# Seven block products for eight in the value projections of a dilated attention

## The chip, the cores and the metric

The kernel runs on one core of one Trainium2 chip. The metric is the time of one execution on the device in microseconds; it is the median of three runs, and less is better.

## The reference

A trunk of two layers over 256 tokens of width 1024, all in float32. Layer 0 mixes the tokens by neighbourhood attention and latent attention, layer 1 by dilated attention; a squared-ReLU MLP follows each. The change lies in layer 1. Cut to it:

```python
def odd_mixer(xn, w_in, w_o, cos_f, sin_f):
    b, s, _ = xn.shape
    hcat = (xn @ w_in).reshape(b, s, DIL_GROUPS, 3, DIL_HEADS, HEAD_DIM)   # 3 groups, q/k/v, 16 heads of 64
    q = apply_rope(hcat[:, :, :, 0], cos_f, sin_f)
    k = apply_rope(hcat[:, :, :, 1], cos_f, sin_f)
    v = hcat[:, :, :, 2]
    return dilated_attention(q, k, v) @ w_o

# dilated_attention: for each group (w, d) of ((128, 1), (512, 4), (2048, 16)) a query attends to the keys
# at offsets -w/2 .. w/2 in steps of d; the three results are combined by their softmax denominators.
```

So each head needs its queries, keys and values in three groups, all of them products of the same normed activations (256 x 1024) with columns of `w_in`.

## The kernel before, in words

A float32 product is made of three faster ones. Each operand is split in two: a high part (`split`: ScalarE casts to float32r, L205) and a low part (VectorE subtracts, L206); `mm3` then adds high x high, high x low and low x high (L209 to L211). Weights come from memory by SP's DMA queue into `raw` tiles (four buffers, `RAWBUFS`), are split in `WPARTS` pieces into `whi` and `wlo` (three buffers each), and are used. `specs` lists all weight tiles in order of use; `weight()` hands out the next one, after it has begun loads up to `LOAD_AHEAD` tiles ahead and splits up to `SPLIT_AHEAD` tiles ahead.

Layer 1 works in eight units of two heads. A unit has three tiles of query and key weights and two of value weights. `qk_steps` makes the query and key products (L927, L928), evacuates them (L934, L935) and applies rope: four DMAs on SP's queue swap halves (`sw`, L942), then VectorE multiplies by cosine (L947) and sine (L948) and adds (L950, L953). Part b = 0 gives the queries and keys of the first group (`q0h`, `q0l`), b = 1 the queries of the other two (`q12`), b = 2 their keys (`k12`). `value_steps` makes the values of the three groups for two blocks of 128 tokens, 384 columns wide and eight blocks of 128 inputs deep: 2 x 8 x 3 matmuls of 128x384. VectorE writes the first group's values (`v0`, L904), ScalarE those of the other two (`v12`, L907, L908).

`attention` of a unit has the scores of the first group (`two_heads`, L218), the strided scores (L981), the softmax (L992 to L997), and transposes (L1004). `mix` multiplies with the values (L1019, L1024). `weave` runs the products of unit u as `main`, with the attention of unit u - 1 as `side` between its steps. A scheduler then sets the order on each engine from this program; each engine runs its own list strictly in that order and waits for the others by semaphores.

The MLPs make their second product by seven products of blocks for eight (`SEVEN`): weights are summed in blocks by DMAs that add to what lies there (POOL's queue, L145) and activations are combined on VectorE.

## Time and profile before

| | |
|---|---|
| median of the runs | 733.81 us (733.56 to 734.0, 3 runs) |
| the profiled execution, its own time | 734.39 us |
| its span in the profile | 732.6 us |
| granted TensorE clock | 0.999 |
| busy in the span: TensorE, VectorE, ScalarE, POOL | 99%, 85%, 71%, 10% |
| moved by DMA | 149.56 MB, 204 GB/s over the span |

A row of an instruction group gives the line, the engine, what is written and read, the shape, the number, then the busy time in us and the mean duration of one in ns, and behind the second bar the idle time ahead of it and what ended that. Rows of TensorE and VectorE can overlap their neighbours by a part of their duration, so the distance from start to start is what one costs. A row of waits has the total in us, the number of times and the longest.

### The profile page before, as it was taken

What the parts mean: (1) busy time and instruction counts of PE and PEld (TensorE: products, weight loads), DVE (VectorE), ACT (ScalarE), POOL (GpSimd) and SP (SyncE); (2) the same over time, 40 slices, a digit from 0 to 9 for tenths busy, and PEclk for the clock granted to TensorE, in tenths of its full rate; (3) what the DMA queues carried; (4) which work ended last, traced back from release to release, by engine and by line L of the source; (5) the groups of instructions that cost most, each with busy time, mean ns of one, the idle gap of its engine ahead of it and who ended that gap; (6) DMA issues with size and microseconds to landing.
All of it is one profiled execution on the core that took longest, in us unless ns stands there. A gap on an engine that the chain in (4) does not pass through costs nothing.

```text
span 732.6 us, 13831 instructions
## 1 busy us (share of the span) xinstructions
PE 723.4 (99%) x5234; PEld 661.0 (90%) x5234; DVE 623.7 (85%) x1188; ACT 521.8 (71%) x985; POOL 75.8 (10%) x73
## 2 busy tenths in 40 slices
PE   9999999999999999999999999999999999999995
PEld 6988899999999998989899899998999999999995
DVE  6888859999999959988777888788759998999956
ACT  7778968767767756877676766867658766776851
POOL 0100002224212000000000000000003132222000
PEclk9999999999999999999999999999999999999999
DMA  8773338799888644664655456455558797898601
GB/s 314 278 260 135 116 115 216 214 283 249 264 265 231 218 160 166 216 211 149 223 181 176 167 187 212 167 187 200 204 190 201 242 271 217 259 272 241 217 32 59
DMA packets 38212, 149.56 MB, mean 204 GB/s; under 512 B 5121, under 2 KB 6657, under 8 KB 29057
## 3 DMA queue, kind: packets, MB, share of 16 engines
q1 hardware_dynamic: 30240, 133.71, 51.6%
q0 software_dynamic: 7616, 14.68, 12.1%
q8 instruction: 41, 0.67, 0.4%
q10 hardware_dynamic: 288, 0.28, 0.1%
q14 instruction: 27, 0.21, 0.1%
HBM read 142.10 MB, written 1.05 MB: 195 GB/s over the span
## 4 chain that ended last, share of the span: by engine, by line
PE 82%; issue 10%; DVE 4%; ACT 1%; DMA 1%; POOL 0%; POOLq 0%; ACTq 0%; DVEq 0%
PE acc L927 11%; PE acc L209 10%; PE acc L210 9%; PE w L209 9%; PE w L210 9%; PE acc L211 9%; PE w L211 9%; PE acc L928 5%; PE w L218 1%; PE w L1004 1%; DVE wlo L206 1%; PE acc L1019 1%; PE w L806 1%; DMA sum<-in_w 1%; PE w L820 1%
## 5 line engine op out<-in xcount | busy, mean ns | idle before, releaser
L206 DVE TENSOR_TENSOR wlo<-raw,whi 128x512 fp32r<-128x512 f32 (+3 forms) x360 | 297.3, 847 | 51.9 <-ACT whi L205 51.8
L205 ACT CAST whi<-raw 128x512 fp32r<-128x512 f32 (+3 forms) x360 | 253.5, 746 | 87.2 <-PE w L210 58.9
L210 PE MATMUL w<-xx,whi 128*128 128x256 f32 x528 | 149.6, 283 | 0.2
L211 PE MATMUL w<-xx,wlo 128*128 128x256 f32 x528 | 149.3, 283 | 0.0
L209 PE MATMUL w<-xx,whi 128*128 128x256 f32 x528 | 148.9, 283 | 0.0
L927 PE MATMUL acc<-xx,whi 128*128 128x512 f32 x336 | 122.1, 404 | 0.0
L210 PEld LDWEIGHTS w<-xx,whi 128*128 128x128 f32 x528 | 101.2, 192 | 1.7 <-DVE xx L246 0.6
L209 PEld LDWEIGHTS w<-xx,whi 128*128 128x128 f32 x528 | 101.0, 192 | 1.1
L211 PEld LDWEIGHTS w<-xx,wlo 128*128 128x128 f32 x528 | 101.2, 192 | 0.0
L928 PE MATMUL acc<-xx,wlo 128*128 128x256 f32 x336 | 94.4, 281 | 0.0
L144 POOL COPY sum<-sum 128x512 f32<-128x512 f32 x28 | 39.3, 1417 | 463.6 <-DMA sum<-in_w 406.6
L927 PEld LDWEIGHTS acc<-xx,whi 128*128 128x128 f32 x336 | 63.1, 188 | 14.2
L928 PEld LDWEIGHTS acc<-xx,wlo 128*128 128x128 f32 x336 | 63.5, 189 | 0.0
L209 PE MATMUL acc<-whi,xx 128*128 128x384 f32 (+2 forms) x160 | 55.9, 351 | 0.0
L210 PE MATMUL acc<-wlo,xx 128*128 128x384 f32 (+2 forms) x160 | 55.4, 346 | 0.0
L211 PE MATMUL acc<-whi,xx 128*128 128x384 f32 (+2 forms) x160 | 54.9, 343 | 0.0
L205 ACT CAST hh<-h 128x896 fp32r<-128x896 f32 (+1 forms) x32 | 28.9, 904 | 24.5 <-DVE h L382 23.7
L209 PE MATMUL w<-whi,hh 128*128 128x512 f32 (+1 forms) x108 | 42.1, 390 | 0.0
L210 PE MATMUL w<-wlo,hh 128*128 128x512 f32 (+1 forms) x108 | 41.5, 384 | 0.0
L211 PE MATMUL w<-whi,hl 128*128 128x512 f32 (+1 forms) x108 | 41.2, 382 | 0.0
L206 DVE TENSOR_TENSOR hl<-h,hh 128x896 fp32r<-128x896 f32 (+1 forms) x32 | 34.8, 1087 | 0.0
L206 DVE TENSOR_TENSOR suml<-sum,sumh 128x1024 fp32r<-128x1024 f32 x28 | 34.4, 1229 | 0.0
(232 smaller groups left out, 1545.6 us busy)
## 6 DMA issues: line engine op xcount, KB each, us to landing
raw<-in_w SPq DMA_DIRECT2D x36, 1024.0 KB, 5.5
raw<-in_w_oqk SPq DMA_DIRECT2D x24, 1024.0 KB, 4.9
raw<-in_w SPq DMA_DIRECT2D x28, 768.0 KB, 4.8
sum<-in_w POOLq DMA_DIRECT2D x28, 512.0 KB, 7.9
raw<-in_w_ov SPq DMA_DIRECT2D x16, 768.0 KB, 4.4
sum<-in_w SPq DMA_DIRECT2D x28, 256.0 KB, 5.9
sw<-qk SPq DMA_DIRECT2D x84, 64.0 KB, 2.4
raw<-in_w_oe SPq DMA_DIRECT2D x4, 1024.0 KB, 5.9
```

Of the source, the lines that this page charges most:

```text
L144: nc.gpsimd.tensor_copy(out=sums[:, 1, :], in_=sums[:, 0, :])
L205: a = nc.scalar.copy(hi, src).ins
L206: return a, (eng or nc.vector).tensor_tensor(lo, src, hi.bitcast(F32), op=ALU.subtract).ins
L209: nc.tensor.matmul(o, sh, mh, start=first, stop=False)
L210: nc.tensor.matmul(o, sh, ml, start=False, stop=False)
L211: nc.tensor.matmul(o, sl, mh, start=False, stop=last)
L218: nc.tensor.matmul(o[j], y[pb, 0, ts], z[pb, 1, :], start=n == 0, stop=n == 2)
L806: nc.tensor.transpose(pt[:, b * P:(b + 1) * P], pp[:, b // 2, (b % 2) * P:(b % 2 + 1) * P], ident)
L820: nc.tensor.matmul(pvo[64 * j:64 * j + 64, 0:P], v[:, kk, h * 64:(h + 1) * 64], pts[:, 2 * j + kk, :], start=kk == 0, stop=kk == NT - 1)
L927: nc.tensor.matmul(two(pq), wh[:, ws], xT[:, k], start=k == 0, stop=False)
L928: nc.tensor.matmul(pq[:, T:2 * T], wl[:, ws], xh[:, k, :], start=False, stop=k == KT - 1)
L1004: nc.tensor.transpose(pt[:, b * P:(b + 1) * P], pp[:, at:at + P], ident)
```

## The change

Values of units 0 and 1 are made as before. Those of units 2 to 7 are made for two units at a time (2 and 3, 4 and 5, 6 and 7). The product of the activations (two blocks of tokens by pairs of input blocks) with the weights of both units is a 2 x 2 product of blocks, made of seven products instead of eight: P1, Q7, P2, Q6 in the even unit (`pair_values`, first list) and Q4, Q5, Q3 in the odd one. Each has 4 x 3 matmuls of 128x384.

- Activations: `combine(b)`, called four times, makes four combined tiles `comb` on VectorE (three of the calls stand in unit 1, one in unit 2).
- Weights: a new array `w_op` holds the four blocks b11, b12, b21, b22 of a pair. P1, P2, Q5 and Q3 take a tile of their own from `raw`, and Q5's gets b12 added by a DMA. Q7, Q6 and Q4 take sums that grow in one held buffer: b12 + b22, then + b11 once Q7's tile has been split, then + b21 once Q6's has. The additions are accumulating DMAs on POOL's queue. While it is held, the `raw` tiles go through three buffers instead of four.
- Value tiles are split in two pieces of 768 columns instead of four of 384.
- Partial sums `t` and `v` are kept in memory (`pt`, `pv`); `place` adds a product to one of them and writes `v0` on ScalarE and `v12` as before.
- For units 0 to 6 the addition of rope's two products for `q12` is made by an accumulating DMA on POOL's queue (L1082 in the new file) instead of VectorE.
- In the even unit P1 and Q7 stand behind the first four steps of the query and key products, not behind the last.

```diff
     for u in range(8):
-        ov = [(a["w_ov"][u, j], 4 * 384, WPARTS, False) for j in range(2)]
-        oqk = [(a["w_oqk"][u, j], WCH, WPARTS, False) for j in range(3)]
-        specs.extend(oqk + ov if u else ov + oqk)
+        oqk = [piece(a["w_oqk"][u, j], WCH, WPARTS) for j in range(3)]
+        if u < 2:
+            ov = [piece(a["w_ov"][u, j], VCH, WPARTS) for j in range(2)]
+            specs.extend(oqk + ov if u else ov + oqk)
+            continue
+        b11, b12, b21, b22 = (a["w_op"][u // 2 - 1, f] for f in range(4))
+
+        if u % 2 == 0:
+            specs.extend(oqk[:1] + [piece(b11, VCH, 2), piece((b12, b22) if u == 2 else None, VCH, 2, held=True, then=(b11,))]
+                         + oqk[1:] + [piece(b21, VCH, 2), piece(None, VCH, 2, held=True, then=(b21,))])
+        else:
+            new = tuple(a["w_op"][u // 2, f] for f in (1, 3)) if u < 7 else ()
+            specs.extend(oqk + [piece(None, VCH, 2, held=True, then=new), piece(b11, VCH, 2, add=b12), piece(b22, VCH, 2)])
...
+    def next_raw(j):
+
+        return (state["raw"] + 1) % (RAWBUFS - (HELD_FROM <= j <= HELD_TO))
...
+    def hold(n, srcs):
+
+        if len(srcs) == 2:
+            state["held"] = raw_place(RAWBUFS - 1)
+            nc.sync.dma_start(state["held"][:, 0:n], srcs[0])
+        if srcs:
+            nc.gpsimd.dma_start(state["held"][:, 0:n], srcs[-1], accum_op=ALU.add)
...
+        if add is not None:
+            nc.gpsimd.dma_start(raw[:, 0:n], add, accum_op=ALU.add)
...
-        return split(hi, lo, raw, eng)
+        done = split(hi, lo, raw, eng)
+        if i == n - 1 and then:
+            hold(width, then)
+        return done
...
+        while HELD_FROM < state["loaded"] <= min(HELD_TO, j + LOAD_AHEAD + 1) and owner.get(next_raw(state["loaded"]), 0) <= j:
+            load_weight()
...
+        def combine(b):
+            g, e = scratch([4, P], "g"), scratch([4, P], "e")
+            for f in range(2):
+                k = 2 * b + f
+                nc.scalar.activation(g[:, 2 * f:2 * f + 2, :], x[:, k, :].rearrange("p (t n) -> p t n", t=2), AF.Copy,
+                                     scale=gains[:, 2 * KT + k:2 * KT + k + 1])
+
+            nc.vector.tensor_tensor(e[:, 2:4, :], g[:, 1:2, :].broadcast_to([P, 2, P]), g[:, 0:4:3, :], op=ALU.subtract)
+            nc.vector.tensor_tensor(e[:, 1, :], g[:, 0, :], e[:, 3, :], op=ALU.subtract)
+            nc.vector.tensor_tensor(e[:, 0, :], g[:, 2, :], e[:, 1, :], op=ALU.subtract)
+            split(*(z[:, b] for z in comb), e)
+
+        def pair_values(first):
...
+            def place(d, i, pq, other, op):
+                c = scratch([384], "c")
+                nc.vector.tensor_tensor(c, pq, other, op=op)
+                nc.scalar.activation(d["v0"][:, i, :], c[:, 0:P], AF.Copy, scale=column(r[0], i))
+                strided_values(d, i, c)
+
+            def p1():
+                nc.scalar.copy(t, product("P1"))
+
+            def q7():
+                nc.vector.tensor_tensor(v, product("Q7"), t, op=ALU.subtract)
+
+            def p2():
+                place(first, 0, product("P2"), t, ALU.add)
+
+            def q6():
+                pq = product("Q6")
+                nc.vector.tensor_tensor(t, pq, t, op=ALU.subtract)
+                nc.vector.tensor_tensor(v, pq, v, op=ALU.add)
+
+            def q4():
+                place(first, 1, product("Q4"), v, ALU.subtract)
+
+            def q5(second):
+                pq = product("Q5")
+                place(second, 1, pq, v, ALU.add)
+                nc.vector.tensor_tensor(t, pq, t, op=ALU.add)
+
+            def q3(second):
+                place(second, 0, product("Q3"), t, ALU.add)
...
+                elif b == 1 and later:
+                    nc.gpsimd.dma_start(r1, sw, accum_op=ALU.add)
...
-        weave(qk_steps(nd) + all_values(nd), attention(0, d, lambda: None, 3), 3)
+        main = qk_steps(nd) + all_values(nd)
+        for at, b in ((3, 0), (8, 1), (13, 2)):
+            main[at:at] = [lambda b=b: combine(b)]
+        weave(main, attention(0, d, lambda: None, 3), 3)
...
+            main = qk_steps(nd, later=u < 7)
+            if u % 2 == 0:
+                now, more_values = pair_values(nd)
+                main[4:4] = now[:2]
+                main += now[2:]
+            else:
+                main += more_values(nd)
+            if u == 2:
+                main[1:1] = [lambda: combine(3)]
```

In the new file `split` stands at L261 and L262, `mm3` at L265 to L267, the query and key matmuls at L1054 and L1055, their evacuation at L1062, rope's swaps at L1069 and its products at L1076 and L1077, `two_heads` at L274, the strided scores at L1112, the accumulations of the held block at L175 and that of Q5's tile at L200. `pq` in `pair_values` is an `acc` bank; `place` is L1008.

TensorE, where the scores of a unit begin, before (unit 2's scores, in unit 3's weave). The strided scores, which read `q12` and `k12`, follow the first group's at once:

```order
L218 MATMUL w_4605<-q0l_4183,q0h_4182 128x256
L218 MATMUL w_4606<-q0l_4183,q0h_4182 128x256
L218 MATMUL w_4605<-q0h_4182,q0l_4183 128x256
L218 MATMUL w_4606<-q0h_4182,q0l_4183 128x256
L981 MATMUL w_4603<-k12_4185,q12_4184 64x64 [waits DVE_49]
```

The same place in the changed kernel. The mixing of the unit before (L1150) follows here instead:

```order
L274 MATMUL w_4658<-q0l_4215,q0h_4214 128x256
L274 MATMUL w_4659<-q0l_4215,q0h_4214 128x256
L274 MATMUL w_4658<-q0h_4214,q0l_4215 128x256
L274 MATMUL w_4659<-q0h_4214,q0l_4215 128x256
L1150 MATMUL acc_4688<-pts_4386,v0_3465 64x128 [waits Activation_49]
```

And this is where the strided scores stand now, behind three pairs of the unit's second query/key tile (`whi_4633`), with 16 pairs of the first one and the mixing ahead of that:

```order
L1055 MATMUL acc_4802<-xx_3347,wlo_4634 128x256
L1054 MATMUL acc_4802<-xx_3347,whi_4633 128x512
L1055 MATMUL acc_4802<-xx_3347,wlo_4634 128x256
L1112 MATMUL w_4656<-k12_4217,q12_4216 64x64 [waits DMASW3_49,DVE_49]
L1112 MATMUL w_4657<-k12_4217,q12_4216 64x64
```

They moved back by 19 pairs, and they now wait for a DMA of POOL's queue (DMASW) beside VectorE.

POOL's list has nothing between the norm of layer 1 and the second MLP before:

```order
L144 COPY sum_3120<-sum_3120 128x512 [waits DMAHW7_49,DMASW2_49,DVE_49]
L145 DMA sum_3120<-in_w2 128x2x512 [waits Pool_49]
L269 TENSOR_TENSOR rstd_3576<-ms_3580,mhalf_92 128x2 [waits DVE_49]
L144 COPY sum_6955<-sum_6955 128x512 [waits DMAHW4_49,DMASW4_49,DMAHW5_49,DVE_49,Activation_49]
L145 DMA sum_6955<-in_w2 128x2x512 [waits Pool_49]
```

Now 19 accumulating DMAs stand there. The first nine, for units 0 to 3 and the first held sum of the second pair (`raw_3816` and `raw_4869` are held blocks, `raw_4643` is Q5's tile):

```order
L175 DMA raw_3816<-in_w_op 128x1536 [waits DMAHW3_49,DMAHW1_49,DMAHW5_49,DMAHW0_49,DVE_49]
L1082 DMA q12_3457<-sw_3737 128x512 [waits DVE_49,PE_49,Activation_49]
L1082 DMA q12_3463<-sw_4032 128x512 [waits DMAHW3_49,DMAHW4_49,DMAHW2_49,DMAHW5_49,DVE_49,PE_49]
L175 DMA raw_3816<-in_w_op 128x1536 [waits DMASW6_49,DVE_49]
L175 DMA raw_3816<-in_w_op 128x1536 [waits DMASW1_49,DVE_49,Activation_49]
L1082 DMA q12_4216<-sw_4494 128x512 [waits DMAHW2_49,DMAHW3_49,DMASW7_49,DMAHW4_49,DMASW3_49,DMAHW5_49,DVE_49,PE_49]
L200 DMA raw_4643<-in_w_op 128x1536 [waits DMAHW3_49,DMAHW1_49,DMAHW6_49,DMAHW0_49,DMAHW7_49,DMASW4_49,Activation_49]
L175 DMA raw_4869<-in_w_op 128x1536 [waits DMASW5_49,DMAHW6_49,DMASW2_49,DVE_49]
L1082 DMA q12_4629<-sw_4854 128x512 [waits DMAHW5_49,DMAHW4_49,DMAHW6_49,DMASW0_49,DMAHW7_49,DVE_49,PE_49]
```

The `q12` of unit 2 (`q12_4216`) is queued behind the third part of the first held sum, and each waits for VectorE.

VectorE at the end of unit 2, before:

```order
L948 TENSOR_TENSOR sw_4402<-sw_4402,sinT_3444 128x512 [waits DMAHW4_49,DMAHW5_49,DMAHW3_49,DMAHW2_49]
L947 TENSOR_TENSOR r1_4477<-qk_4429,cosT_3443 128x512 [waits DVE_49]
L953 TENSOR_TENSOR q12_4184<-r1_4403,sw_4402 128x512 [waits DVE_49]
L206 TENSOR_TENSOR wlo_4513<-raw_4417,whi_4512 128x512 [waits Activation_49]
L904 TENSOR_SCALAR v0_4186<-acc_4497,rstd_3576 128x128 [waits PE_49]
```

and now, from Q6's split (`wlo_4574`, of the held block) on:

```order
L262 TENSOR_TENSOR wlo_4574<-raw_3816,whi_4573 128x768 [waits DMASW1_49,PE_49]
L1062 TENSOR_TENSOR qk_4517<-acc_4518,low_4535 128x256 [waits PE_49,Activation_49]
L262 TENSOR_TENSOR wlo_4574<-raw_3816,whi_4573 128x768
L1062 TENSOR_TENSOR qk_4517<-acc_4538,low_4561 128x256 [waits Activation_49]
L262 TENSOR_TENSOR wlo_4603<-raw_4445,whi_4602 128x512 [waits DMAHW0_49,PE_49]
L262 TENSOR_TENSOR wlo_4603<-raw_4445,whi_4602 128x512 x2
L262 TENSOR_TENSOR wlo_4603<-raw_4445,whi_4602 128x512 [waits Activation_49]
L1077 TENSOR_TENSOR sw_4494<-sw_4494,sinT_3444 128x512 [waits DMAHW4_49,DMAHW5_49,DMAHW3_49,DMAHW2_49]
```

Q6's split waits for the DMA that added b11, and the addition for `q12` is gone; the last evacuations of the unit's queries and keys and rope's product stand behind that split.

More of the change, by code (lines that the diff above doesn't have):

```diff
@@ L45 @@
 WPARTS = 4
+VCH = 4 * 384
 NORM_PRIO = 300
@@ L133, in trunk, with raw_place, raw_tile @@
     parts = {}
-    state = {"loaded": 0, "split": (0, 0), "used": 0, "pool": None, "parts_done": None}
+    state = {"loaded": 0, "split": (0, 0), "used": 0, "pool": None, "parts_done": None, "raw": 0, "held": None}
+    sums_at = [j for j, z in enumerate(specs) if z[5]]
+    HELD_FROM, HELD_TO = sums_at[0] - 5, sums_at[-1]
+    owner = {}
+    def next_raw(j):
+        return (state["raw"] + 1) % (RAWBUFS - (HELD_FROM <= j <= HELD_TO))
+    def raw_place(i):
+        return wraw.tile([P, WCH], F32, tag=f"raw{i}", name="raw", bufs=1)
+    def raw_tile(j):
+        state["raw"] = next_raw(j)
+        owner[state["raw"]] = j
+        return raw_place(state["raw"])
+    def hold(n, srcs):
[4 more added lines that the diff above has]
+            nc.gpsimd.dma_start(state["held"][:, 0:n], srcs[-1], accum_op=ALU.add)
     def load_weight(pieces=1, before=lambda i: None):
         j = state["loaded"]
-        src, n, _, seven = specs[j]
+        src, n, _, seven, add, held, _ = specs[j]
+        state["loaded"] = j + 1
+        if j == HELD_FROM + 1:
+            hold(VCH, specs[sums_at[0]][0])
+        if held:
+            parts[j] = [None, None, None]
+            return
         if seven:
@@ L146, in load_weight @@
             n = 3 * BLK
-        raw = wraw.tile([P, WCH], F32, tag="raw", name="raw")
+        raw = raw_tile(j)
         for i in range(pieces):
@@ L160, in split_piece @@
         j, i = state["split"]
-        _, _, n, seven = specs[j]
+        _, width, n, seven, _, held, then = specs[j]
         state["split"] = (j, i + 1) if i < n - (not seven) else (j + 1, 0)
@@ L915, in qk_steps @@
+        def qk_steps(d, wide=True, later=True):
             hold = {}
```

50 lines of the change are left out of this document (37 added, 13 removed).

## The prediction

> **What bounds the kernel now.** I read the page first: busy shares, the granted clock, the chain that ended last.
>
> ```profile
> span 732.6 us, 13831 instructions
> ...
> PE 723.4 (99%) x5234; PEld 661.0 (90%) x5234; DVE 623.7 (85%) x1188; ACT 521.8 (71%) x985; POOL 75.8 (10%) x73
> ...
> PEclk9999999999999999999999999999999999999999
> ...
> PE 82%; issue 10%; DVE 4%; ACT 1%; DMA 1%; POOL 0%; POOLq 0%; ACTq 0%; DVEq 0%
> ```
>
> TensorE is busy for 99% of the span at full clock and is 82% of the chain. The page averages over stages, so I went on to the stage of the change. Three consecutive units of the dilated attention, and a stretch of the first MLP for comparison, from the busy times by window (PE, PEld, DVE, ACT, POOL, then clock, DMA share and GB/s):
>
> ```profile
> 404.83:434.56 29.73, 29.73 (x235) 27.07 (x234) 24.41 (x62) 21.38 (x51) 0.00 (x0) 1.00 0.56 186
> 434.56:464.29 29.73, 29.73 (x235) 27.06 (x234) 24.40 (x62) 21.36 (x51) 0.00 (x0) 1.00 0.56 187
> 464.29:494.01 29.72, 29.72 (x234) 27.05 (x234) 24.39 (x62) 21.36 (x51) 0.00 (x0) 1.00 0.56 187
> ...
> 404.83:464.29 59.46, 59.46 (x467) 54.13 (x466) 48.81 (x123) 42.73 (x101) 0.00 (x0) 1.00 0.56 187
> 150.00:200.00 50.00, 50.00 (x330) 46.07 (x330) 49.13 (x61) 34.89 (x44) 15.70 (x10) 1.00 0.93 264
> ```
>
> A unit takes 29.73 us, and TensorE works in all of it; VectorE is busy for 24.4 us, so 5.3 us are spare. Fewer matmuls therefore shorten a unit until VectorE or the DMA engines stop it. The MLP row shows how far that has gone elsewhere: VectorE at 98% and DMA at 0.93, TensorE still without a gap. Last, the waits in the two units 404.83 to 464.29 (total, times, longest):
>
> ```profile
> DVE wlo L206 <- ACT whi L205: 6.4, 4, 2.2
> DVE drz L996 <- ACT pp L995: 2.8, 2, 1.4
> PEld w L218 <- issue: 0.7, 3, 0.2
> ```
>
> TensorE waits for no engine there. VectorE's waits fill its spare time; of them the 1.4 us per unit for the exponential ahead of the reciprocal is a dependence inside the softmax, which I keep.
>
> **The matmuls removed.** A value product is a run of 128x384 matmuls. First and last of 19 that follow each other without a gap:
>
> ```profile
> 399.99 0.33 PE L211 MATMUL acc<-whi,xx 128*128 128x384 f32 x1
> ...
> 403.11 0.33 PE L211 MATMUL acc<-whi,xx 128*128 128x384 f32 x1
> ```
>
> 18 starts in 3.12 us: 0.173 us each, though a row lasts 0.33 (they overlap). A pair of units had 8 block products of 4 x 3 matmuls, and has 7: 96 become 84. Three pairs lose 36 matmuls, 36 x 0.173 = 6.2 us. All of it falls in the odd units: the even one keeps four products (29.73 us), the odd one has three (29.73 - 2.08 = 27.65 us).
>
> **The work added on VectorE and ScalarE.** Durations, from the groups of 404.83 to 464.29 by shape, and four subtractions in a row from the timeline:
>
> ```profile
> L206 DVE TENSOR_TENSOR wlo<-raw,whi 128x512 fp32r<-128x512 f32 x24 | 15.8, 686 | 6.4 <-ACT whi L205 6.4
> L206 DVE TENSOR_TENSOR wlo<-raw,whi 128x384 fp32r<-128x384 f32 x16 | 8.5, 552 | 0.0
> L935 DVE TENSOR_TENSOR qk<-acc,low 128x256 f32<-128x256 f32 x12 | 5.0, 418 | 0.2
> L904 DVE TENSOR_SCALAR v<-acc,rstd 128x128 f32<-128x128 f32 x4 | 1.4, 346 | 0.0
> L205 ACT CAST whi<-raw 128x512 fp32r<-128x512 f32 x25 | 13.9, 618 | 1.7 <-DMA sw<-qk 0.8 <-PE acc L927 0.8
> L205 ACT CAST whi<-raw 128x384 fp32r<-128x384 f32 x16 | 7.4, 514 | 2.9 <-PE acc L927 2.9
> L934 ACT COPY low<-acc 128x256 f32<-128x256 f32 x12 | 4.3, 362 | 2.5 <-PE acc L928 2.5
> L907 ACT ACTIVATE v<-acc,rstd 64x128 f32<-64x128 f32 x8 | 2.9, 362 | 1.1 <-DVE v L904 1.0
> ...
> 405.13 2.49 DVE L206 TENSOR_TENSOR wlo<-raw,whi 128x512 fp32r<-128x512 f32 x4
> ```
>
> Four 512-wide subtractions take 2.49 us, so one costs the engine (2.49 - 0.69) / 3 = 0.60, 0.086 below its mean. I take 0.086 off each mean: 0.47 for 384 columns, 0.33 for 256, 0.26 for 128. A 768-wide one is in no row: by the line through 384 and 512 columns its mean is 0.954, its cost 0.87; two of 384 (0.93) are the upper end, 0.87 the lower, since a fixed part is saved once. I take 0.87; the upper end would add 14 x 0.06 = 0.9 us a pair.
>
> - Even unit: eight splits of 768 for eight of 384, 8 x (0.87 - 0.47) = +3.2; one 384-wide combination for two 128-wide scalings, 0.47 - 0.52 = -0.05; Q7 and Q6's three additions, +1.4; q12's addition gone to a DMA, -0.6. Sum +4.0: 24.4 becomes 28.4 of 29.73.
> - Odd unit: six splits of 768 for eight of 384, +1.5; three combinations for two scalings, +0.9; Q5's update of t, +0.5; q12, -0.6. Sum +2.2: 26.6 of 27.65.
> - Combined activations, four times: 0.33 + 2 x 0.26 + 0.60 = 1.45. Three fall in unit 1: 24.4 + 4.35 - 0.6 = 28.2, which with the 1.4 of waiting fits under 29.73. The fourth falls in unit 2, which is already at 28.4.
> - ScalarE, per pair: 14 casts of 768 (0.83 by its own two rows) for 16 of 0.51, +3.5; P1's copy, about 0.5; four scalings of v0, under 4 x 0.36: 42.7 becomes 48.1 of 57.4 us. The 9 us left cover it. Each combined tile costs ScalarE two 256-wide scalings and a cast, 2 x 0.36 + 0.62 = 1.3: three of them, 4.0, against the 8.4 us that a unit leaves it.
>
> With the softmax's 1.4 us the even unit needs 28.4 + 1.4 = 29.8, 0.1 over; the odd one 28.0, 0.35 over. Three pairs: 3 x 0.45 = 1.35. Unit 2 adds 1.45. Unit 7 keeps its q12 addition, 0.6. Sum given back: 3.4 us. If splits fill the softmax's wait, nearly nothing is given back; if the other waits stay as well, a unit is as long as before or longer.
>
> **The DMAs added**, with the queues, the accumulating transfers and the swaps of rope as they are today:
>
> ```profile
> q1 hardware_dynamic: 30240, 133.71, 51.6%
> q0 software_dynamic: 7616, 14.68, 12.1%
> ...
> sum<-in_w POOLq DMA_DIRECT2D x28, 512.0 KB, 7.9
> raw<-in_w_ov SPq DMA_DIRECT2D x16, 768.0 KB, 4.4
> ...
> 419.52 2.41 SPq L942 DMA_DIRECT2D sw<-qk  x4
> ...
> DMA to landing us min/median/max: 6.4/7.9/12.2
> ...
> DMA to landing us min/median/max: 1.9/2.4/5.6
> ```
>
> (The first landing row is that of the accumulating transfers, L145, the second that of the swaps, L942.) Queue 1 needs 51.6% of 732.6 us for 133.71 MB, 2.83 us per MB; queue 0, which accumulates, 6.04. A pair now loads five value blocks for four (+0.79 MB, 2.2 us) and accumulates four blocks of 0.79 MB and two q12 of 0.26 MB (3.67 MB, 22.2 us). Today's share is 0.56 x 59.46 = 33.3 us, so 57.7 us of DMA stand against 57.4 of TensorE. These prices hold packets that were slowed by each other; the windows above reach 0.93 at most. So DMA has no slack left by this price, and enough if packets go faster than their mean. I cost it at nothing in the sum: the loads are issued up to four tiles ahead, and the MLP ran at 0.93 without a gap.
>
> The Trainium skill, DMA: Bandwidth & Descriptors, section "Anatomy of one DMA — SWDGE (gpsimd) path", gives such a transfer 2.0 us and 436 GB/s. By it the 3.67 MB would be an estimated 8.4 us and the pair's DMA 44 us, with no question left. The trace disagrees: 14.68 MB in 12.1% of the span is 166 GB/s.
>
> **The waits added.** The first is on TensorE: L1112, the strided scores, waits for q12's accumulation, and everything behind it in TensorE's order waits too, the query/key matmuls of the unit first. In units 3, 5 and 7 that transfer stands on POOL's queue behind the one that adds b21 to the held block, which starts when Q6's split is done. The cover on TensorE from there, with these pieces of the chain of waits:
>
> ```profile
> 434.10 0.12 PE acc L928
> 434.21 0.23 PE acc L927
> ...
> 434.56 0.91 PE w L218 x10
> ...
> 436.09 0.59 PE acc L1019 x8
> 436.68 0.23 PE acc L1024 x8
> 436.91 0.44 PE acc L1019 x8
> 437.35 0.23 PE acc L1024 x8
> ```
>
> P2 and Q6, 24 x 0.173 = 4.2; 19 pairs of query/key matmuls at 0.35, 6.7; scores 0.9; mix 1.5: 13.2 us. The b21 block (0.26 MB more than today's 512 KB) lands after 7.9 + 0.26 x 6.04 = 9.5, q12 1.6 behind it: 11.1. The bounds are 6.4 (the fastest row, for a third of the bytes or more) and 12.2 + 3.2 = 15.4 (the slowest). I take 11.1, from the median: hidden, no cost.
>
> The second is on VectorE: Q6's split waits until b11 has been added to the block that Q7's split has read, and behind it stand rope's products and the evacuations of queries and keys. Between the two splits TensorE has P1 and Q7 (4.2) and 32 query/key pairs (11.2), 15.4 us, less the two halves of the split itself, 1.7: 13.7 against 9.5, at the slowest 13.8. Hidden.
>
> The third is the tightest: Q5's tile is b11 loaded by SP, then b12 added. SP issues that load behind the swaps of the third rope of the even unit, hence when the even unit's query/key products are done, about when Q6's split is; four swaps take SP 2.4 us, the load 4.4, the addition 9.5: 16.3. Its split stands on VectorE behind the first three softmax pieces of the odd unit, which themselves wait for L1112: 13.2, then Q4's split (1.7) and nine pieces of 64 to 384 columns (about 3.3): 18 us. Between 12.6 (fastest) and 20.6 (slowest) I take 16.3: hidden by 1.9 us. Behind it on VectorE stand the last reciprocal and the odd unit's first evacuation, which TensorE needs for its accumulators.
>
> On SP the load that begins the next pair's held block waits for Q4's last split, and rope's swaps of the odd unit are queued behind. That split stands on VectorE ahead of the evacuations that those swaps need, so it is done earlier: no cost.
>
> **Sum.** -6.2 + 3.4 = -2.8. The profiled execution's own time is 734.39 (its span 732.6 and 1.8 around it), 0.6 above the median of 733.81; it would become 731.6, and the median 731.0.
>
> **Rivals.**
> 1. All cover holds (the MLP's case): the splits fill the softmax's wait, -6.2, 727.6. For it: VectorE at 98% there. Against: the MLP has no softmax in which VectorE and ScalarE wait for each other in turn.
> 2. New waits for accumulating DMAs take the gain, at L1112 or at Q5's split. Each is 2 us late at the slowest row (15.4 against 13.2, 20.6 against 18); halfway, one of them is late by 1.1 in each of the three odd units, 3.3 on top of the forecast: 734.3, no change. For it: the 12.2 was seen beside a DMA share of 0.93, and the odd units are to have as much. Against: the median leaves 1.9 us at both.
> 3. The DMA engines become the bound, the one that ends slower: if they sustain no more than the MLP's 0.93, a pair takes 57.7 / 0.93 = 62.0 us, 2.6 more than 59.46, and three pairs 7.7: 741.5. It decides at a share of 57.7 / 59.46 = 0.97: above, the change still gains. For it: the tiles go through three raw buffers now instead of four. Against: nothing in the trace shows 0.93 to be a ceiling, and TensorE did not wait at it.
>
> That the change does nothing is no rival: the order shows 36 matmuls fewer.
>
> **Chances.** Forecast 0.44 (its own range 727.6 to 732.3), rival 1 0.10, rival 2 0.18, rival 3 and lateness of both kinds together 0.28. A change below 0.2% (1.5 us) is about what this kernel's measurement cannot tell from none. Faster: 0.54; same 0.18; slower 0.28. The range runs from full cover, 727.4, to 740.0, which leaves out the worse half of rival 3.
>
> **What would show it.** Right: odd units of 27.7 to 28.5 us, even ones near 29.8, VectorE at 95% in both, unit 2 the longest, TensorE's waits below 2 us in any one unit and for wlo. Rival 2: TensorE idle ahead of L1112 until a DMA. Rival 3: DMA share at 0.9 or more with casts and splits waiting for raw. Wrong altogether: units beyond 30 us with VectorE waiting for rope's swaps or the held block in its own order.

## The result: 777.4 us, 6.0% slower

The changed kernel takes 777.38 us (median of four, 775.6 to 779.49) against 733.68 (733.53 to 734.0) for the kernel before on the same chip: ratio 1.060 [1.057, 1.062]. 731.0 was forecast, with 727.4 to 740.0 as the range. Of all the runs below, one execution (782.3 us, of the kernel with POOL's subtractions and the weights' additions) was in a slower state of the chip and is left out of its median. The page of the changed kernel, its lines in the order of those of before:

```profile
span 773.8 us, 13905 instructions
...
PE 736.9 (95%) x5198; PEld 666.9 (86%) x5198; DVE 646.5 (84%) x1202; ACT 543.8 (70%) x1007; POOL 94.4 (12%) x92
...
PEclk9999999999999999999989999899999999999999
...
q1 hardware_dynamic: 30672, 136.07, 50.1%
q0 software_dynamic: 10352, 25.96, 19.8%
...
PE 67%; DMA 12%; issue 10%; DVE 8%; ACT 2%; POOL 0%; POOLq 0%; DVEq 0%; SPq 0%; ACTq 0%
```

TensorE issues the 36 matmuls fewer (5198 for 5234), and yet is busy for longer. DMA was 1% of the chain that ended last and is 12%; VectorE was 4% and is 8%; the clock row has two 8s.

All of the loss lies in the stage of the change. From its first query/key matmul to the first matmul of the second MLP, in the busy times by window of the kernel before (PE, PEld, DVE, ACT, POOL, then clock, DMA share and GB/s):

```profile
315.01:552.18 237.17, 236.97 (x1906) 216.89 (x1905) 190.93 (x471) 167.82 (x387) 3.49 (x6) 1.00 0.56 189
```

and of the changed kernel, the whole stage and three of its units:

```profile
314.85:593.42 278.57, 250.60 (x1870) 222.60 (x1869) 213.49 (x485) 189.69 (x409) 18.47 (x23) 0.94 0.73 210
...
349.58:380.57 30.99, 30.47 (x233) 26.97 (x233) 28.57 (x66) 23.13 (x50) 1.73 (x2) 1.00 0.67 192
380.57:420.10 39.53, 31.57 (x215) 27.14 (x214) 25.40 (x60) 20.07 (x43) 2.58 (x3) 0.87 0.73 194
488.26:526.46 38.20, 34.77 (x240) 30.91 (x239) 31.80 (x69) 30.38 (x67) 3.03 (x4) 0.91 0.68 189
```

The stage is 41.4 us longer. TensorE is idle for 278.57 - 250.60 = 28.0 us of it, where it was idle for 0.2. It is also busy for 13.6 us more with fewer matmuls: a mean clock of 0.94 over 278.57 us is 16.7 us of lost full-speed time (some 15, because a part of the slow time passes while TensorE stands still), the matmuls left out are -6.2, and what remains, 3 to 5 us, fits gaps too short to count as idle. Over the whole stage neither VectorE nor the DMA engines are full: VectorE is busy for 77% of it, the DMA share is 0.73. The average hides short stretches that are full: in the 8 us behind the issue of a `q12` addition, taken for units 1 to 6, the DMA share is 0.92 to 1.02.

Some of the waits between 300 and 570 us (total, times, longest):

```profile
...
PE w L1112 <- DMA q<-sw: 17.7, 6, 5.1
...
DVE sn L1123 <- PE w L1112: 11.3, 5, 5.7
...
ACT whi L261 <- DMA raw<-in_w_oqk: 9.2, 2, 5.1
ACT whi L261 <- DMA raw<-in_w_op: 8.8, 3, 3.4
...
DVE sw L1077 <- DMA sw<-qk: 4.8, 3, 2.6
```

The first row is the strided scores' wait for the `q12` addition. The two rows of ScalarE are casts that wait for weights in `raw`, 18.0 us together; by the view of L200, 5.6 of them are for the additions to Q5's tile, and by that of L175 nothing waits for the held block's. The longest wait for `q12`, in the chain of waits between 452 and 464 us:

```profile
451.60 0.70 DVE sw L1077
452.29 0.03 POOLq L1082
452.32 0.50 issue
452.82 0.01 POOLq L200
452.83 10.40 DMA q<-sw
463.23 0.14 issue
463.37 0.66 PE w L1112 x13
```

VectorE's sine product is done at 452.29, POOL issues the addition half a microsecond later, and its 256 KB land after 10.40 us. TensorE, in its timeline around that place:

```profile
457.53 0.40 PE L1054 MATMUL acc<-xx,whi 128*128 128x512 f32 x1
457.77 0.28 PE L1055 MATMUL acc<-xx,wlo 128*128 128x256 f32 x1
457.89 0.39 PE L1054 MATMUL acc<-xx,whi 128*128 128x512 f32 x1
...
463.37 1.13 PE L1112 MATMUL w<-k,q 64*64 64x64 f32 x32 [5.08 <-DMA q<-sw]
...
464.81 0.63 PE L1054 MATMUL acc<-xx,whi 128*128 128x512 f32 x1
465.23 0.41 PE L1055 MATMUL acc<-xx,wlo 128*128 128x256 f32 x1
465.45 0.63 PE L1054 MATMUL acc<-xx,whi 128*128 128x512 f32 x1
```

Ahead of the wait a pair of query/key matmuls starts every 0.36 us (457.53 to 457.89), behind it every 0.64 (464.81 to 465.45). The wait is paid twice: 5 us of standing still, and then work at half the clock. Two windows around and behind such waits, from the same view as above (the granted clock, 0.51 and 0.65, is the third figure from the end):

```profile
403.00:410.00 7.00, 5.63 (x18) 4.56 (x19) 4.95 (x10) 3.28 (x9) 0.86 (x1) 0.51 0.78 168
...
463.45:470.00 6.55, 6.55 (x54) 5.70 (x55) 4.55 (x18) 3.69 (x9) 0.86 (x1) 0.65 0.67 123
```

The Trainium skill, TensorE: Matmul & The Clock Gate, section "What's actually happening", has the clock fall to half after an idle window of about 3.4 us and come back after as long a busy one. The trace of the changed kernel agrees roughly: in this stage the clock halved behind each of the seven gaps of 2.4 to 5.5 us between two matmul starts, and behind none of up to 1.6. Two runs below show that the length alone does not decide: behind a gap of 2.1 us the clock fell in the kernel with the products spread out (0.67 from 391.8 to 397 us), behind one of 3.3 us it did not in the kernel without the weights' additions (1.00 from 450 to 457 us).

### The profile page after: what moved, and what is told of

The parts are those of the page before. It is cut to its first block, busy times and chain, and to the rows that moved or that the text cites. A ratio compares the mean times of both kernels' runs of the same rounds, so it can differ in the third digit from the quotient of the medians.

```text
span 773.8 us, 13905 instructions
## 1 busy us (share of the span) xinstructions
PE 736.9 (95%) x5198; PEld 666.9 (86%) x5198; DVE 646.5 (84%) x1202; ACT 543.8 (70%) x1007; POOL 94.4 (12%) x92
## 4 chain that ended last, share of the span: by engine, by line
PE 67%; DMA 12%; issue 10%; DVE 8%; ACT 2%; POOL 0%; POOLq 0%; DVEq 0%; SPq 0%; ACTq 0%
PE w L265 9%; PE w L266 9%; PE w L267 9%; PE acc L265 8%; PE acc L266 8%; PE acc L267 8%; PE acc L1054 7%; DMA q<-sw 5%; DMA raw<-in_w_op 5%; PE acc L1055 3%; DVE wlo L262 3%; DMA sum<-in_w 1%; ACT whi L261 1%; PE w L862 1%; PE w L1135 1%
## 5 line engine op out<-in xcount | busy, mean ns | idle before, releaser
L262 DVE TENSOR_TENSOR wlo<-raw,whi 128x512 fp32r<-128x512 f32 (+4 forms) x354 | 311.4, 897 | 53.9 <-ACT whi L261 53.6
L261 ACT CAST whi<-raw 128x512 fp32r<-128x512 f32 (+4 forms) x354 | 266.0, 788 | 126.5 <-PE w L266 72.3
L267 PE MATMUL w<-xx,wlo 128*128 128x256 f32 x528 | 149.3, 283 | 0.0
L265 PE MATMUL w<-xx,whi 128*128 128x256 f32 x528 | 148.9, 283 | 0.0
L1054 PE MATMUL acc<-xx,whi 128*128 128x512 f32 x336 | 131.4, 426 | 1.3 <-DVE qk L1062 1.0
L265 PEld LDWEIGHTS w<-xx,whi 128*128 128x128 f32 x528 | 101.0, 192 | 1.1
L267 PEld LDWEIGHTS w<-xx,wlo 128*128 128x128 f32 x528 | 101.2, 192 | 0.0
L1055 PE MATMUL acc<-xx,wlo 128*128 128x256 f32 x336 | 99.4, 296 | 1.3 <-DVE wlo L262 1.3
L1054 PEld LDWEIGHTS acc<-xx,whi 128*128 128x128 f32 x336 | 68.1, 203 | 17.6 <-DVE qk L1062 1.4
L191 POOL COPY sum<-sum 128x512 f32<-128x512 f32 x28 | 41.4, 1495 | 258.6 <-DMA sum<-in_w 165.6
L1055 PEld LDWEIGHTS acc<-xx,wlo 128*128 128x128 f32 x336 | 68.5, 204 | 2.0 <-DVE wlo L262 1.8
L265 PE MATMUL w<-whi,hh 128*128 128x512 f32 (+1 forms) x108 | 42.1, 390 | 0.0
L267 PE MATMUL w<-whi,hl 128*128 128x512 f32 (+1 forms) x108 | 41.2, 382 | 0.0
L261 ACT CAST hh<-h 128x896 fp32r<-128x896 f32 (+1 forms) x32 | 28.9, 903 | 12.6 <-DVE h L438 12.5
L262 DVE TENSOR_TENSOR hl<-h,hh 128x896 fp32r<-128x896 f32 (+1 forms) x32 | 36.0, 1124 | 0.0
L265 PE MATMUL acc<-whi,xx 128*128 128x384 f32 (+2 forms) x100 | 35.4, 358 | 0.1
L266 PE MATMUL acc<-wlo,xx 128*128 128x384 f32 (+2 forms) x100 | 35.3, 353 | 0.0
L267 PE MATMUL acc<-whi,xx 128*128 128x384 f32 (+2 forms) x100 | 34.9, 349 | 0.0
L262 DVE TENSOR_TENSOR suml<-sum,sumh 128x1024 fp32r<-128x1024 f32 x28 | 34.4, 1228 | 0.0
```

The costliest lines, as they stand in the source:

```text
L191: nc.gpsimd.tensor_copy(out=sums[:, 1, :], in_=sums[:, 0, :])
L261: a = nc.scalar.copy(hi, src).ins
L262: return a, (eng or nc.vector).tensor_tensor(lo, src, hi.bitcast(F32), op=ALU.subtract).ins
L265: nc.tensor.matmul(o, sh, mh, start=first, stop=False)
L266: nc.tensor.matmul(o, sh, ml, start=False, stop=False)
L267: nc.tensor.matmul(o, sl, mh, start=False, stop=last)
```

## The experiments

Each is a small edit of the changed kernel unless it says otherwise. Two theories stood at first: the `q12` addition, on TensorE's path, costs most (A), or the twelve additions of weights do (B); a third, that the rest is VectorE's (C), came in by what was left. Later groups of runs have theories of their own, and a letter then means what the expectation beside it says. Most kernels with accumulating DMAs differ by 4 us or more from execution to execution, and five kernels ran only once, so a price below holds to a few microseconds.

### The two kinds of accumulating DMA

`q12` added on VectorE again; the weights' additions stay:

```diff
-        def qk_steps(d, wide=True, later=True):
+        def qk_steps(d, wide=True, later=False):
...
-            main = qk_steps(nd, later=u < 7)
+            main = qk_steps(nd)
```

> The changed kernel with the addition for q12 back on VectorE in every unit; all else as changed. Theory A (the strided scores wait for the accumulating DMA of q12; each wait of 3 us or more is followed by a stretch at half clock): both go, 41 us less, about 733 to 742 us. Theory B (the added weight DMAs, 25% of queue time, make raw tiles and the held block late; the wait for q12 is only where TensorE happens to stand): waits move to casts and splits, 755 us or more. Theory C (VectorE is too full): slower than the changed kernel, since VectorE gets 0.6 us more per unit.

Measured: 764.88 us (762.55 to 766.67), ratio 1.041 [1.039, 1.044]; 12.5 below the changed kernel. So `q12` is a part of the loss and not most of it, as theory B had it. The converse, the kernel before with nothing but the `q12` additions made by DMA (`r1` is the tile of `q12` there):

```diff
+                elif b == 1 and later:                     # units 0 to 6
+                    nc.gpsimd.dma_start(r1, sw, accum_op=ALU.add)
```

> The kernel before with only the addition for q12 of units 0 to 6 made by the accumulating DMA on POOL's queue. Today the strided scores start 5.7 to 8.1 us after rope's sine product. Theory A1 (the DMA takes 6 to 10 us by itself, whatever else runs): the scores wait in most units, 745 us or more. Theory A2 (it takes that long only beside the weight additions): it lands in under 6 us and the time is within 2 us of before, 732 to 736.

Measured: 735.29 us (733.72 to 737.27), ratio 1.001 [1.000, 1.003]. In its stage the addition lands in about half the time (KB each, median us):

```profile
q<-sw POOLq DMA_DIRECT2D x7, 256.0 KB, 3.9
```

against this in the changed kernel:

```profile
q<-sw POOLq DMA_DIRECT2D x7, 256.0 KB, 7.6
```

The same transfer is harmless here. Next the weights' additions are left out and those of `q12` stay, and then both are left out:

```diff
-            nc.gpsimd.dma_start(state["held"][:, 0:n], srcs[-1], accum_op=ALU.add)
...
-            nc.gpsimd.dma_start(raw[:, 0:n], add, accum_op=ALU.add)
```

> The changed kernel without the twelve accumulating DMAs that sum weight blocks (the held block and Q5's tile keep one plain block each, so the values of units 2 to 7 are other numbers); the addition for q12 stays a DMA. Theory A2: q12 lands in 4 to 6 us, waits at the strided scores mostly go, under 745 us. Theory A1: they stay, 760 us or more.

> The changed kernel without any accumulating DMA in the attention: q12 added on VectorE and weight blocks not summed (other numbers for the values of units 2 to 7). What is left is the seven products, the extra splits and combinations, and three raw buffers. Theory A and B: 728 to 733 us, since TensorE has 6.2 us less to do. Theory C (VectorE too full): 736 us or more, with TensorE waiting for wlo.

Measured: 752.70 and 742.34 us, one run each. So `q12` costs 10.4 without the weights' additions and 12.5 with them; the weights' additions cost 22.5 without `q12` and 24.7 with it. And 742.3 is still 8.2 above the kernel before (734.1 beside it), 14.4 above what the matmuls should give; that much is left for theory C.

The 752.70 corrects theory A2, by which `q12` lands late only beside the weights' additions. Without them it still does (KB each, median us):

```profile
q<-sw POOLq DMA_DIRECT2D x7, 256.0 KB, 6.8
```

What goes with the slow landing is how busy the DMA engines are at that moment, and not their average: in the 8 us from the issue of the addition their share is 0.83 to 0.96 in units 1 to 6 here, and 0.57 to 0.65 in units 2 to 6 of the kernel before with `q12` by DMA (0.91 in its unit 1), though the share of the whole stage is about 0.6 in both.

Of the weights' additions alone, the nine into the held buffer and the three into Q5's tile were left in by turns, `q12` on VectorE in both:

> q12 added on VectorE, the held block's nine additions stay, the three additions to Q5's tile are left out (other numbers for the values of units 3, 5 and 7). The weight sums cost 22 us together. Theory B1 (Q5's tile, a load and an addition in a row, is what comes late, as the prediction called it the tightest): 744 to 750 us. Theory B2 (the load on the DMA engines makes everything late, three additions of twelve take a quarter away): 757 to 762 us.

> q12 added on VectorE, the three additions to Q5's tile stay, the held block keeps one plain block (other numbers for the values of units 2 to 7). Theory B1: 758 us or more. Theory B2: 745 to 750 us.

Measured: 755.52 and 754.46 us, one run each, each about half way. Three additions to Q5's tile cost as much as nine to the held buffer, so the count of bytes alone doesn't set the price; neither expectation was right.

### What is left without any accumulating DMA

Theory C says that VectorE comes late. Its subtractions of the paired value tiles were moved to POOL, first without, then with the weights' additions:

```diff
-        done = split(hi, lo, raw, eng)
+        done = split(hi, lo, raw, nc.gpsimd if width == VCH and n == 2 else eng)
```

> As the kernel without any accumulating DMA (742.3 us; values of units 2 to 7 are other numbers), but the 42 subtractions that make the low parts of the paired value tiles run on POOL, which is idle there: 12 us less on VectorE per pair. Theory C (what is left of the loss is VectorE being nearly full, with the softmax in its order): 728 to 734 us. Theory D (it is the split buffers: value tiles use up three buffers in half the time, and casts wait for TensorE): no gain, 740 us or more.

> As the kernel with q12 added on VectorE (764.9 us, the weight sums still by DMA), with the same 42 subtractions on POOL. Theory C alone: 750 to 757 us, the 22 us of the weight sums stay. If the weight sums only cost because VectorE had no slack to catch up after a late tile: below 742 us. POOL's DMA starts now stand between subtractions, which may make them later: above 765 us.

Measured: 757.94 (one run), and 776.46 us (median of four, 770.1 to 779.48); 15.6 and 11.6 slower than their controls. A reason shows in rope's sine product, which has two inputs in memory (minimum, median, maximum in ns). With the subtractions on VectorE, and then on POOL:

```profile
L1073 DVE TENSOR_TENSOR sw<-sw,sinT x18: 680/687/696, 364.7 to 532.1; 128x512 f32<-128x512 f32 x18
```

```profile
L1073 DVE TENSOR_TENSOR sw<-sw,sinT x17: 677/1150/2339, 365.8 to 539.3; 128x512 f32<-128x512 f32 x17
```

VectorE's own work became longer while POOL read memory: without its 42 subtractions it is busy for 218.2 us of the stage, with them for 214.6. So the test did not relieve VectorE and says nothing about C. (The Trainium skill, SBUF — State Buffer, section "Who interferes with whom": a VectorE instruction with two inputs in SBUF contends with a POOL instruction that reads it. The trace agrees.) A cleaner one leaves these subtractions out and lets the matmuls read the high part twice; beside it the products were spread out, and a fourth pair of split buffers was tried against its control, both without the block sums of the activations:

```diff
+        if width == VCH and n == 2:                       # no subtraction
+            parts[j][2] = parts[j][1]
...
+                main[8:8] = now[1:2]                       # spread: P1 and Q7 apart
+                main[4:4] = now[:1]
...
+                main[4:4] = more[:1]                       # and Q4 early
...
+            ring = 3 + (HELD_FROM <= j <= HELD_TO)         # four split buffers
```

> The kernel with no accumulating DMA at all (742.3 us), and now the low part of the paired value tiles is not subtracted either: VectorE's 42 subtractions of 128x768 (about 1.1 us each, 46 us in six units) are left out, and the matmuls that read the low part read the high part in its place, so their number and shape stay. Theory C (the 14 us over the matmuls' account are VectorE's: it is 27 of 30 us busy and comes late): 728 to 733. Theory D (three split buffers for thirteen tiles instead of ten; ScalarE waits in its own order for a buffer to come free, and the probabilities wait behind it): 738 to 743, since the buffers and ScalarE's copies stay. Theory B (products in bursts, a weight tile for every 2.1 us of TensorE where there was one for 4.2): between them, 732 to 738, since ScalarE's half of the burst stays.

> The same kernel with the products spread out: Q7 after the second tile of queries and keys instead of straight after P1, and Q4 after the first such tile of the odd units instead of after all three; same instructions, other places. Theory B: 732 to 738. Theories C and D: 740 to 746, since the work of VectorE and the number of tiles in the ring are the same; the queries and keys have 2.1 us less matmul between them and their scores in odd units, which can cost some us.

> The kernel with no accumulating DMA, without the block sums of the activations (the sums' products read plain blocks; this frees 16 KB a partition), and with a fourth pair of split buffers in the paired units. To be read against the next one, which has three. Theory D: 6 to 14 us below it, at 728 to 735. Theory C: within 3 us of it. Theory B: 3 to 8 below it, as one tile more can be split ahead of a burst.

> The control of the one before: no accumulating DMA, without the block sums of the activations, three pairs of split buffers as before. VectorE and ScalarE lose four combinations of about 2 us each in the first three units. All theories: 737 to 742; under C nearer to 737.

Measured: 732.76 us (732.3 to 733.55); 742.24 (741.29 to 745.38); 736.45 (735.96 to 737.11); 731.0 (730.7 to 732.2), ratio of the last 0.996 [0.994, 0.997]. The first is what C gave, the last is what no theory gave: without the block sums the full load of subtractions does no harm. A fourth buffer, in an order that changed with it, made it slower by 5.4, and spreading the products changed nothing (742.24 for 742.34): nothing speaks for theory D or for bursts (B here). The stage of the control, three buffers:

```profile
314.79:548.87 234.08, 233.56 (x1870) 211.30 (x1869) 208.55 (x474) 184.21 (x399) 3.48 (x6) 1.00 0.59 202
```

VectorE is busy for 208.55 of 234.08 us, 89%, and TensorE idles for 0.5. The stage is 3.1 us shorter than before: -6.2 for the matmuls, and +3.1 that fits small gaps, none of them longer than 1.2 us from start to start.

The four combinations of activations stand in units 1 and 2, but the kernel that has them loses its time in units 4 to 6 as well. Leaving anything out also changes the order in which the scheduler writes what remains. So the same instructions were run in three other orders, by moving the combinations, and the whole changed kernel in one:

```diff
-        for at, b in ((3, 0), (8, 1), (13, 2)):
+        for at, b in ((3, 0), (8, 1), (13, 2), (18, 3)):   # all in unit 1; then late; then early
```

> The kernel with no accumulating DMA (742.3 us), whole otherwise, with the fourth combination of activations moved from unit 2 to the end of unit 1. The same instructions; the scheduler writes them in another order: 111 of ScalarE's 942, 151 of VectorE's 1190 and 137 of TensorE's 3439 stand elsewhere. Theory O (the 14 us over the matmuls' account are the order in which the scheduler happens to put the splits, the softmax and the evacuations, and not the amount of work): any of these three orders can fall between 731 and 746, and they differ from each other by over 4 us. Theory W (it is the amount of work that the block sums add on VectorE, ScalarE and their scratch): 740 to 744.5 for all three.

> The same with the three combinations of unit 1 moved later in it (behind steps 10, 15 and 17 instead of 3, 7 and 11): 31 of ScalarE's, 101 of VectorE's and 92 of TensorE's instructions stand elsewhere than in the kernel of 742.3 us. Theory O: 731 to 746, and away from the other two. Theory W: 740 to 744.5.

> The same with all four combinations in the first half of unit 1: 32 of ScalarE's, 50 of VectorE's and 72 of TensorE's instructions stand elsewhere. The least changed order of the three. Theory O: 731 to 746, nearer to 742 than the others. Theory W: 740 to 744.5.

> The changed kernel whole (777.4 us), its accumulating DMAs too, with the fourth combination moved as in the first of these: 40 of ScalarE's, 144 of VectorE's and 96 of TensorE's instructions stand elsewhere. If the 35 us that the accumulating DMAs cost are of the DMAs themselves (theory A): 771 to 783. If they too are an order that fits badly (theory O taken to the whole): below 765 is possible.

Measured: 739.74 (739.38 to 740.11), 744.35 (743.84 to 744.86), 743.64 (743.56 to 743.73), and for the whole 772.32 us (767.07 and 777.57), two runs each. Units 4 and 5 in the order of 742.3:

```profile
402.54:437.68 35.14, 34.65 (x251) 30.58 (x250) 32.23 (x69) 29.70 (x65) 0.00 (x0) 1.00 0.56 192
437.68:468.57 30.89, 28.36 (x221) 24.84 (x221) 25.57 (x59) 21.17 (x44) 0.00 (x0) 1.00 0.60 218
```

and in that of 739.7:

```profile
404.92:436.70 31.78, 31.78 (x240) 28.26 (x239) 31.33 (x69) 28.78 (x65) 0.00 (x0) 1.00 0.55 188
436.70:463.60 26.90, 26.90 (x209) 23.51 (x208) 23.62 (x56) 18.82 (x42) 0.00 (x0) 1.00 0.59 193
```

The same two units take 66.0 us in one order and 58.7 in the other, though the first holds 23 matmuls more, since the scores slide along the products; the second order pays elsewhere. Order is worth 4.6 us in these four kernels, and some 9 to 13 us above the control without block sums stay in all of them. Neither theory alone holds: what the block sums cost is not settled further. The whole changed kernel stays slow in its other order, far above the 765 that it could have fallen below if the order were the cause; so the 35 us between 777.4 and 742.3 are for the most part of the DMAs themselves.

### The weights' additions in one order: wait or traffic

Into the control of 731.0 us the weights' twelve additions were put back, once where the splits wait for them, once into two buffers aside that nobody reads. TensorE's order is the same in all three kernels; in the second, VectorE's and ScalarE's too.

```diff
+        nc.gpsimd.tensor_copy(out=state["aside"][i % 2][:, 0:1], in_=after)          # starts it when the real one would
+        nc.gpsimd.dma_start(state["aside"][i % 2][:, 0:n], src, accum_op=ALU.add)
```

> The kernel of 731.0 us (no block sums of the activations, no accumulating DMA; TensorE's gaps over 0.6 us in the stage sum to 0.65 us) with its twelve weight additions by accumulating DMA put back where the changed kernel has them, so that the splits wait for them. TensorE's order is that of the kernel of 731.0, word for word; 13 of ScalarE's 928 and 17 of VectorE's 1176 instructions stand elsewhere. The earlier difference of two kernels with and without these additions was 22.5 us, in orders that also differed. Theory A (they cost as a wait or as traffic, in any order): 748 to 757. Theory O (in a good order the cover that was forecast holds): 731 to 736.

> The same with the twelve additions made into two buffers aside that nobody reads, each begun when the real one would be (behind a copy of one column on POOL from the tile that it waits for); the weights that are used are loaded as in the kernel of 731.0, and the orders of TensorE, VectorE and ScalarE are exactly its own. What leaves the sum out is the held and Q5's weights. If the additions cost as traffic that slows loads, swaps and other transfers: as the run before it, or within 4 us of it. If they cost as waits, a split behind an addition that lands late: 730 to 735.

Measured: 749.08 us (746.53 to 752.61), ratio 1.019 [1.015, 1.023], and 746.02 (745.15 to 747.46), ratio 1.016 [1.015, 1.018]. Additions that nobody waits for cost 15.0 us; the waits add 3.1, with ranges that overlap. So in this order traffic alone is enough for most of the price. That does not make the waits cheap by themselves: where the splits wait, weight transfers into `raw` have 11.7% of the chain that ended last between 314 and 575 us and the swaps 6.0%; with the additions aside the swaps have 13.3%. That fits two late paths side by side, of which a kernel without the one still has the other; no run here takes the traffic away and keeps the waits. The waits in the kernel with the additions aside:

```profile
DVE sw L1072 <- DMA sw<-qk: 16.1, 6, 7.3
ACT q0h L266 <- DVE r L1074: 12.7, 6, 5.1
ACT pp L1121 <- DVE dmn L1118: 12.0, 6, 3.5
```

and its DMA issues (KB each, median us to landing):

```profile
raw<-in_w_op SPq DMA_DIRECT2D x15, 768.0 KB, 5.8
aside<-in_w_op POOLq DMA_DIRECT2D x12, 768.0 KB, 9.3
...
sw<-qk SPq DMA_DIRECT2D x84, 64.0 KB, 4.1
```

In the control, the same two views:

```profile
DVE sw L1060 <- DMA sw<-qk: 4.4, 4, 1.7
```

```profile
raw<-in_w_op SPq DMA_DIRECT2D x15, 768.0 KB, 5.0
...
sw<-qk SPq DMA_DIRECT2D x84, 64.0 KB, 2.7
```

Rope's swaps of 64 KB land 1.4 us later, and VectorE waits 16.1 us for them instead of 4.4, with the evacuations and the softmax queued behind it in order. The weight loads, 0.8 us later, have tiles of lead, and the casts wait only 2.8 us for them. (The Trainium skill, DMA: Bandwidth & Descriptors, section "Queues, rings and completion order": each DMA engine takes turns between the queues that have work, a packet at a time. The slower swaps beside a second queue agree with it; no run here shows single turns.)

## Why the prediction was wrong, step by step

| part | forecast, us | measured, us | from |
|---|---|---|---|
| matmuls removed | -6.2 | -6.2 | 36 fewer, 0.17 each in the stage |
| work on VectorE and ScalarE | +3.4 | +3.1, and +11.3 (9 to 13) with the block sums | 731.0 against 734.1; 739.7 to 744.4 against 731.0 |
| weights' additions | 0 | +22.5; in another kernel and order +15.0 as traffic, +3.1 as waits | 764.88 - 742.34; 746.0 and 749.1 against 731.0 |
| `q12`'s addition | 0 | +12.5 | 777.38 - 764.88 |

With the kernel before at 733.7 to 734.1 these make up the 777.4; the parts were taken out one behind the other, so each price holds in that order of taking out.

- **The matmuls** were right, in number and price.
- **VectorE's account** was right as work: a 128x768 subtraction has a mean of 0.956 us in the control (0.954 was forecast), and VectorE runs at 89% with no harm. That +3.4 and +3.1 lie so close is partly luck. The control has no fourth combination (1.45 less) and keeps `q12`'s additions on VectorE (0.6 more in each of five more units), which is +5.0 by the prediction's own prices; and its units 4 and 5 take 31.65 and 26.71 us where 29.8 and 28.0 were forecast. That the control's time is the forecast 731.0 is chance. The step that failed here is the block sums, "1.45" each. As busy time they fit (VectorE is busy for 214.6 us of the stage with the four of them and 208.55 without, 1.5 each); but the order that the scheduler then writes has TensorE waiting for probabilities and evacuations by up to 1.6 us at a time, and the sum had no term for that. How much belongs to the order and how much to the work stays open.
- **"I cost it at nothing in the sum: the loads are issued up to four tiles ahead"** is the largest failure. The bandwidth sum beside it (57.7 us of DMA for 57.4 of TensorE) compares averages, and on average the engines were not full: the share was 0.73 in the stage and 0.84 in the fullest unit. The sum had no term for what a transfer does to the others in flight. In the one-order pair these were rope's swaps, which have no lead: VectorE's products stand right behind them and waited 16.1 us. In the changed kernel the loads' lead did not hold either: casts waited 18.0 us for `raw` and VectorE 4.8 for swaps; with `q12` on VectorE it is 13.4 and 12.8. Rival 3 had the sign and the casts that wait; its mechanism, DMA engines too slow for a whole pair, is not what was seen, since they were full only for short stretches.
- **"q12 1.6 behind it: 11.1 ... hidden, no cost"** failed twice. The transfer was not short behind another (1.6) but took 7.6 in the median and 10.40 at the place shown; from the start of the b21 addition there (446.78) to its landing (463.23) were 16.4 us, more than the 15.4 named as the slowest. And the cover was counted from Q6's split, 13.2 us, though the addition can begin only with VectorE's sine product, which the order excerpt ahead of the prediction has behind that split: 452.29, with L1112 due at about 458, 5.7 us. Rival 2 named the place and "TensorE idle ahead of L1112 until a DMA"; its price of 3.3 us was a quarter of the true one.
- **No term for the clock.** The seven gaps of 2.4 us and more were followed by half speed: 15 to 17 us of the 41.4, beside 28.0 of idle time. Here a wait term of that length should have been given about half as much again.
- **The second wait** (Q6's split for the held block) was hidden as forecast: no instruction of the changed kernel waits for L175. **The third** (Q5's split) was not: casts waited 5.6 us for L200, in two of the three pairs, and in the runs with a part of the additions the three to Q5's tile cost as much as the nine others.
- The signs named ahead told rightly: units beyond 30 us (30.4 to 39.5), TensorE idle at L1112, casts waiting for `raw`, VectorE waiting for swaps.

## What to carry to other kernels

Before a transfer is costed at nothing because loads have lead, look for the transfers without lead on the same DMA engines: here a 64 KB swap whose consumer waits right behind it paid for bulk traffic at a mean DMA share of 0.76. Look at the share in the microseconds in which a transfer flies, and not at its mean over a stage. Count the cover of a moved addition from its own last input, not from the work that it is queued behind. A TensorE wait of several microseconds can cost more than its length: here 28.0 us of idle time brought 15 to 17 us in slow matmuls. In a program whose order a scheduler writes, a part left out changes the order of the rest, so a part's price needs the same order on both sides, or several orders.

## What was not expected of the hardware

- An accumulating DMA of 256 KB within SBUF lands in 3.9 us (median) in one kernel and in 6.8 to 7.6 (at most 10.4) in two others with about the same or a somewhat higher mean DMA share (0.6, 0.6 and 0.73). The share in the 8 us from its issue tells them apart: 0.57 to 0.65 (0.91 once), against 0.83 to 1.02.
- POOL's subtractions of 128x768 stretch VectorE's two-input products from 0.69 us to 1.15 in the median and 2.34 at most.
- In the changed kernel TensorE's clock halves behind gaps of 2.4 to 5.5 us and stays so for several microseconds: the pairs of matmuls take 0.64 us for 0.36. In other runs it halved behind 2.1 us and did not behind 3.3.
